# Layer norms centre half of their columns on VectorE, weight casts are queued behind the norm's last copy, and the first tile's transposes come one stretch of products later

## The chip, the cores and the metric

The kernel runs on one core of a Trainium2 chip. The metric is the device time of one execution in microseconds; the times shown are a median of three runs. One further execution was recorded by the hardware profiler, and every duration below is from that one.

## The reference

Two transformer blocks run one after the other on 256 tokens of width 1024, all in float32:

- Block 1: RMS norm, one wide input projection, three kinds of attention (sliding window, top-k sparse, memory cross attention), a gated merge, the output projection, then RMS norm, an MLP with squared ReLU (1024 to 4096 to 1024), and a final RMS norm.
- Block 2, layer A: feed-forward (SwiGLU, 1024 to 2816 to 1024), layer norm, a chunked gating unit ("sgu"), layer norm, feed-forward, layer norm. Layer B: keys and values of sparse attention are made ("kv"), feed-forward, layer norm, sparse attention ("nsa"), layer norm, feed-forward, layer norm.

```python
def layer_norm(x, g, b):
    mu = jnp.mean(xf, axis=-1, keepdims=True)
    var = jnp.mean(jnp.square(xf - mu), axis=-1, keepdims=True)
    y = (xf - mu) * lax.rsqrt(var + LN_EPS)
    return y * g + b

def post_norm(x, sub, g, b):
    return layer_norm(DN_ALPHA * x + sub, g, b)
```

Each sublayer of block 2 ends in `post_norm`, six in all; the last one is the output.

## The kernel before

**Numbers.** Every product is made of three: a float32 operand is split into a high part `h` (cast to fp32r, on ScalarE) and a low part `l` (the rest, subtracted on VectorE), and `mm3` (L273) multiplies h·h, h·l and l·h on TensorE.

**Weights.** `Stream` (L95) brings 512 KB halves of weight blocks through five raw buffers, on SP's DMA queue. `prep` (L130) casts a half on ScalarE (L142) and then subtracts on VectorE (L149); a raw buffer comes free only when both have read it. Nine pairs of high and low buffers hold prepared halves. `pump` prepares ahead as far as it is told.

**Sublayers as generators.** The 256 tokens are two tiles of 128 rows. A sublayer is a Python generator with four stops before its last products: it asks for its first weights; it makes its first products for row tile 0; the same for row tile 1; then all its middle (from `W.pump()` on), up to the last products. `down_last` (L313) makes those for one row tile: first the older weight blocks over all 1024 columns, then the last two blocks in three stretches, columns 0 to 511, 512 to 767 and 768 to 1023, so that the norm's statistics can begin on the first columns. A stretch of 256 columns is 12 products.

**The boundary.** `weave` (L426) binds the end of one sublayer, the norm and the beginning of the next. `A(t)` is the norm of row tile t, `B(t)` its transposes (TensorE, L799, two of 128x128 for each 256 columns) with the split of the result into `xT` (ScalarE L331, VectorE L332). Its order for TensorE is written by hand up to the end of the previous sublayer: last products of tile 0, then those of tile 1, in which `B(0)` is put in where `down_last` yields. After that a planner with its own model of costs orders each engine, and `A` and `B` have a higher priority than what is around them. There are eight boundaries: two with `rms_bound` (L762, entirely on VectorE) and six with `ln_bound` (L816), of which the last has no `B`.

**The layer norm.** `A(t)` of `ln_bound` adds the residual and takes statistics on VectorE in three column groups, makes -mean (L831) and the root's input (L832), and then, while VectorE computes the inverse root in small steps (`rsqrt`, L336), ScalarE subtracts the mean (L835) and GpSimd multiplies by the gain (L836), 256 columns at a time. VectorE then multiplies by the root and adds the bias (L850). In all but the last norm all four groups of columns go that way; in the last, three do and one is centred by VectorE (L840), inside the root, in steps that `rsqrt` takes from the generator `centre`.

**What is queued behind what.** The middle of the next sublayer is traced inside `issue_after(end.ins)` (L446). `end` is the last instruction of `B(1)`, VectorE's L332, and `issue_after` puts every instruction that the block traces on that instruction's engine behind it. ScalarE's instructions of the block have no such edge. The block's ScalarE instructions are the weight casts from the third weight block on, the activations, and the DMAs issued on ScalarE's queue: among them the sgu's `sgu_w_s` (L929, 512 KB, transposed by TensorE at L933 right after the first row products) and the small weights `cmp_w2` of the kv stage (L1067, L1069).

Of the kernel before, what the change touches and what calls it, by code (L numbers as in the profile page):

```python
# [23 lines left out]
F32 = mybir.dt.float32  # L24
# [42 lines left out]
def consts():  # L67
    f = np.float32
    p = np.arange(128)[:, None]
    j = np.arange(128)[None, :]  # L70
    cols, parts, n = {}, [], 0
    tri = np.where(j <= p, 0.0, BIG)
    upper = np.where(j > p, 0.0, BIG)
    dist = 255 - np.arange(384)
    nf = np.maximum(dist, 1).astype(f)
    large = 16 + (np.log(nf / f(16)) / f(math.log(8)) * f(16)).astype(np.int32)
    bucket = np.where(dist < 16, dist, np.minimum(large, 31))
    hot = np.zeros((128, 384))
    hot[:32] = (np.arange(32)[:, None] == bucket[None, :]) & (dist >= 0)[None, :]
    for name, a in (  # L80
        ("ident", p == j),
        ("tril_t", p <= j),
        ("rowok", p <= 96),
        ("swa", np.concatenate([tri, upper, tri], 1)),
        ("causal", np.concatenate([tri, np.zeros((128, 128)), tri], 1)),
        ("inv", np.power(10000.0, -np.arange(32) / 32.0)[None, :].repeat(128, 0)),
        ("hot", hot),
    ):
        cols[name] = (n, n + a.shape[1])
        parts.append(a.astype(f))  # L90
        n += a.shape[1]
    return np.ascontiguousarray(np.concatenate(parts, 1)), cols
# [84 lines left out]
class Ker:  # L177
# [135 lines left out]
    def down_last(self, ws, hs, acc, t):  # L313

        ts = slice(t * 128, (t + 1) * 128)
        m = len(ws) - 2
        for w, (hh, hl) in zip(ws[:m], hs):
            self.down(w, hh, hl, acc, t, False, False)
        if t:
            self.W.pump(2)  # L320
        for n, c0, c1 in ((0, 0, 512), (1, 0, 256), (1, 256, 512)):
            ns = slice(n * 512 + c0, n * 512 + c1)
            for i, (w, (hh, hl)) in enumerate(zip(ws[m:], hs[m:])):
                for k, (wh, wl) in enumerate(w):
                    self.mm3(acc[t][n][:, c0:c1], hh[:, k, ts], hl[:, k, ts], wh[:, 0, ns], wl[:, 0, ns], False,
                             i == 1 and k == 1, skip_group_check=c0 > 0)
            if t and n == 0:
                yield

    def split(self, h, l, x):  # L330
# [95 lines left out]
    def weave(self, prev, A, B, nxt):  # L426

        with self.manual(mybir.EngineType.PE):
            next(prev)
            self.first(A, 0)  # L430
            next(prev)
            self.first(B, 0)
            next(prev)
        if nxt:
            next(nxt)
        self.first(A, 1)
        if nxt:
            next(nxt)
        end = self.first(B, 1)
        if not nxt:  # L440
            return
        next(nxt)
        if self.dry:
            next(nxt)
        else:
            with self.tc.issue_after(end.ins):  # L446
                next(nxt)

    def first(self, f, t):
# [340 lines left out]
    def cols(self, rows, t, x):  # L790

        nc = self.nc
        xh, xl = x
        ts = slice(t * 128, (t + 1) * 128)
        for h in range(4):
            ps = self.bank()
            for j in range(2):
                k = 2 * h + j
                nc.tensor.transpose(ps[:, j * 128:(j + 1) * 128], rows[:, k * 128:(k + 1) * 128], self.ident)  # L799
            ks = slice(2 * h, 2 * h + 2)  # L800
            end = self.split(xh[:, ks, ts], xl[:, ks, ts], ps[:, :256].rearrange("p (k s) -> p k s", k=2))
        return end

    def bcast(self, row, name):
# [11 lines left out]
    def ln_bound(self, R, acc, layer, i, scale, last=False):  # L816

        nc, I = self.nc, self.I
        X = self.big([128, 2, D])
        xT = None if last else self.new_xT()  # L820
        gB, bB = (self.bcast(I[v][layer, i:i + 1], n) for v, n in (("ln_g_2", "gB"), ("ln_b_2", "bB")))

        def A(t):
            x = X[:, t]

            def part(c0, c1):
                nc.vector.scalar_tensor_tensor(x[:, c0:c1], R[:, t, c0:c1], ALPHA / scale,
                                               acc[t][c0 // 512][:, c0 % 512:(c1 - 1) % 512 + 1], op0=OP.mult, op1=OP.add)

            mv, nh, nm = self.stats(x, D, part), self.small(name="nh"), self.small(name="nh")  # L830
            nc.vector.tensor_scalar(nm, mv[:, 0:1], -1.0, None, op0=OP.mult)  # L831
            nc.vector.tensor_scalar(nh, mv[:, 1:2], -0.5 * NR, -0.5 * NR * LN_EPS / scale ** 2, op0=OP.mult, op1=OP.add)  # L832
            m = 3 if last else 4
            for cs in self.cuts[:m]:
                nc.scalar.activation(x[:, cs], x[:, cs], AF.Identity, bias=nm)  # L835
                nc.gpsimd.tensor_mul(x[:, cs], x[:, cs], gB[:, cs])  # L836

            def centre():
                for cs in self.cuts[m:]:
                    nc.vector.scalar_tensor_tensor(x[:, cs], x[:, cs], mv[:, 0:1], gB[:, cs], op0=OP.subtract,  # L840
                                                   op1=OP.mult)
                    yield

            y, = self.rsqrt([nh], centre())
            for j, cs in enumerate(self.cuts):
                if last and (t == 0 or j >= 3):
                    nc.scalar.activation(x[:, cs], x[:, cs], AF.Copy, scale=y)
                    nc.gpsimd.tensor_add(x[:, cs], x[:, cs], bB[:, cs])
                else:
                    nc.vector.scalar_tensor_tensor(x[:, cs], x[:, cs], y, bB[:, cs], op0=OP.mult, op1=OP.add)  # L850
                if last and j % 2:
                    hs = slice(j * 256 - 256, j * 256 + 256)
                    nc.sync.dma_start(self.out[0, t * 128:(t + 1) * 128, hs], x[:, hs])

        def B(t):
            if not last:
                return self.cols(X[:, t], t, xT)

        return A, B, X, xT

    def ffn(self, x, layer, i, acc, hooks={}):
# [706 lines left out]
def program(nc, arrays, stop=None):  # L1568
    aps = {}
    for name, a in arrays.items():  # L1570
        aps[name] = nc.dram_tensor(f"in_{name}_dram", a.shape, mybir.dt.from_np(a.dtype), kind="ExternalInput").ap()
    out = nc.dram_tensor("out_0_dram", (1, S, D), F32, kind="ExternalOutput").ap()
    _, cols = consts()
    C = aps.pop("consts")
    specs = Ker(Null(), Null(), aps, C, cols, out, None).run(stop)
    with tile.TileContext(nc) as tc:
        Ker(tc, nc, aps, C, cols, out, specs).run(stop)
# [11 lines left out]
```

## Time and profile before

| | |
|---|---|
| median of 3 runs | 1503.89 us (1502.61 to 1505.08) |
| the profiled execution | 1501.12 us, span 1499.2 us |
| TensorE (PE) busy | 97% of the span |
| VectorE (DVE), ScalarE (ACT), GpSimd (POOL) busy | 64%, 50%, 4% |
| granted TensorE clock, mean | 0.995 of full speed |

In the rows, PE is a product and PEld its weight load; L-numbers are lines of the kernel; an arrow `out<-in` gives the names of the tiles; a bracket at the end of a row of a timeline is the idle time of the engine before it and what ended it. A row with x4 merges four instructions of one kind, and its duration goes from the start of the first to the end of the last. "ACTq" is an instruction that ScalarE's sequencer issues, such as a DMA.

The boundaries with a norm and transposes lie at about 228, 412, 602, 750, 942, 1183 and 1295 us; the last norm is the end of the program.

### The profile page before, as it was taken

The numbers are of one execution on the slowest core, as the hardware profiler recorded it, in microseconds if no ns is written. First come the engines' busy times: TensorE is split into PE (matmuls) and PEld (weight loads), VectorE is DVE, ScalarE is ACT, GpSimd is POOL, SyncE is SP. The second block draws the span as 40 slices with busy tenths as digits, with TensorE's granted clock in tenths as the row PEclk, the third lists the DMA queues.
The fourth block names the chain that finished last, engine by engine and source line by source line (L and its number), as shares of the span: only waits on it lengthen the run. The fifth ranks groups of instructions, "written<-read, shape, count | busy, mean of one in ns | idle before, by whom it ended". The sixth has DMA issues, their size and how long they took to land.

```text
span 1499.2 us, 25253 instructions
## 1 busy us (share of the span) xinstructions
PE 1449.9 (97%) x10093; PEld 1331.4 (89%) x10093; DVE 960.0 (64%) x1608; ACT 747.5 (50%) x1149; POOL 54.3 (4%) x71
## 2 busy tenths in 40 slices
PE   6899999999999999999999999999999999999997
PEld 6688988989899999799889999899999798799996
DVE  7884398555584455877785545876645688665545
ACT  5565565444454443544354443564544487454442
POOL 0000000000000000100010000100000111100002
PEclk9999999999999999999999999999999999999999
DMA  8453276665566665577556665466766352185650
GB/s 295 128 160 91 75 243 225 224 193 185 155 198 194 184 186 165 180 222 246 159 185 186 187 193 173 146 192 218 236 194 186 109 180 85 58 265 180 187 169 29
DMA packets 191714, 264.81 MB, mean 177 GB/s; under 512 B 11024, under 2 KB 159852, under 8 KB 191596
## 3 DMA queue, kind: packets, MB, share of 16 engines
q1 hardware_dynamic: 183068, 249.56, 53.1%
q10 hardware_dynamic: 8528, 13.64, 2.9%
q8 instruction: 79, 1.29, 0.4%
q14 instruction: 39, 0.32, 0.1%
HBM read 262.09 MB, written 1.07 MB: 176 GB/s over the span
## 4 chain that ended last, share of the span: by engine, by line
PE 83%; DVE 8%; ACT 4%; DMA 3%; issue 1%; POOL 0%; ACTq 0%; DVEq 0%; SPq 0%
PE acc L311 20%; PE u L275 17%; PE u L277 17%; PE u L276 17%; DVE wl L149 3%; ACT wh L142 2%; PE acc L276 2%; PE acc L277 2%; PE acc L275 2%; PE acc L695 2%; DVE big L850 1%; PE u L799 1%; DMA wr<-in_ffn_w_dram 1%; PE acc L681 1%; PE u L1516 1%
## 5 line engine op out<-in xcount | busy, mean ns | idle before, releaser
L149 DVE TENSOR_TENSOR wl<-wr,wh 128x1024 fp32r<-128x1024 f32 (+3 forms) x488 | 572.0, 1183 | 417.5 <-ACT wh L142 415.2
L142 ACT CAST wh<-wr 128x1024 fp32r<-128x1024 f32 (+3 forms) x488 | 493.3, 1018 | 562.9 <-PE u L276 225.0
L275 PE MATMUL u<-big,wh 128*128 128x256 f32 x1960 | 551.4, 281 | 1.6 <-ACT med L412 1.1
L277 PE MATMUL u<-big,wl 128*128 128x256 f32 x1960 | 550.0, 281 | 0.0
L276 PE MATMUL u<-big,wh 128*128 128x256 f32 x1960 | 549.6, 280 | 0.0
L275 PEld LDWEIGHTS u<-big,wh 128*128 128x128 f32 x1960 | 369.3, 188 | 4.8 <-ACT med L412 1.3
L276 PEld LDWEIGHTS u<-big,wh 128*128 128x128 f32 x1960 | 368.4, 188 | 2.2
L277 PEld LDWEIGHTS u<-big,wl 128*128 128x128 f32 x1960 | 369.0, 188 | 0.0
L311 PE MATMUL acc<-wh,t 128*128 128x512 f32 x928 | 263.9, 395 | 0.0
L311 PEld LDWEIGHTS acc<-wh,t 128*128 128x128 f32 x928 | 169.8, 188 | 34.9
L311 PE MATMUL acc<-wl,t 128*128 128x512 f32 x464 | 145.6, 394 | 0.0
L311 PEld LDWEIGHTS acc<-wl,t 128*128 128x128 f32 x464 | 87.1, 188 | 20.5
L275 PE MATMUL u<-wh,big 128*128 128x256 f32 (+1 forms) x304 | 101.6, 334 | 0.5 <-ACT t L1429 0.5
L277 PE MATMUL u<-wh,big 128*128 128x256 f32 (+1 forms) x304 | 101.1, 333 | 0.0
L276 PE MATMUL u<-wl,big 128*128 128x256 f32 (+1 forms) x304 | 100.4, 330 | 0.0
L836 POOL TENSOR_TENSOR big<-big,med 128x256 f32<-128x256 f32 x46 | 38.1, 859 | 1387.4 <-ACT big L835 1354.0
L331 ACT CAST t<-t 128x512 fp32r<-128x512 f32 x66 | 41.0, 621 | 56.1 <-DVE t L536 24.3
L275 PEld LDWEIGHTS u<-wh,big 128*128 128x128 f32 x304 | 57.8, 190 | 6.8 <-ACT t L1429 0.9
L277 PEld LDWEIGHTS u<-wh,big 128*128 128x128 f32 x304 | 57.7, 190 | 5.5
L276 PEld LDWEIGHTS u<-wl,big 128*128 128x128 f32 x304 | 57.8, 190 | 5.3
L332 DVE TENSOR_TENSOR t<-t,t 128x512 fp32r<-128x512 f32 x66 | 45.4, 687 | 14.3 <-ACT t L331 14.3
L276 PE MATMUL acc<-wl,t 128*128 128x512 f32 (+1 forms) x168 | 53.9, 321 | 0.3 <-DVE wl L149 0.3
(256 smaller groups left out, 1365.5 us busy)
## 6 DMA issues: line engine op xcount, KB each, us to landing
wr<-in_ffn_w_dram SPq DMA_DIRECT2D x264, 512.0 KB, 4.3
wr<-in_w_in_dram SPq DMA_DIRECT2D x34, 512.0 KB, 3.9
wr<-in_w_mlp_in_dram SPq DMA_DIRECT2D x32, 512.0 KB, 4.5
wr<-in_w_mlp_out_dram SPq DMA_DIRECT2D x32, 512.0 KB, 4.2
wr<-in_sgu_w_in_dram SPq DMA_DIRECT2D x32, 512.0 KB, 4.9
wr<-in_sgu_w_out_dram SPq DMA_DIRECT2D x16, 512.0 KB, 4.7
wr<-in_kv_w_dram SPq DMA_DIRECT2D x12, 512.0 KB, 4.0
wr<-in_w_out_dram SPq DMA_DIRECT2D x8, 512.0 KB, 4.6
```

The costliest lines, as they stand in the source:

```text
L142: self.nc.scalar.copy(h, v)
L149: self.nc.vector.tensor_sub(l, v, h.bitcast(F32))
L275: mm(out, lh, rh, start=start, stop=False, **k)
L276: mm(out, lh, rl, start=False, stop=False, **k)
L277: mm(out, ll, rh, start=False, stop=stop, **k)
L311: mm(acc[t][n], a[:, k, ts], b[:, 0, n * 512:(n + 1) * 512], start=s, stop=e)
L331: self.nc.scalar.copy(h, x)
L332: return self.nc.vector.tensor_sub(l, x, h.bitcast(F32))
L681: nc.tensor.transpose(pt[:, c:c + 128], e[:, c:c + 128], self.ident)
L695: nc.tensor.matmul(out, PT[:, c:c + 128], v(b), start=b == 0, stop=b == nb - 1)
L799: nc.tensor.transpose(ps[:, j * 128:(j + 1) * 128], rows[:, k * 128:(k + 1) * 128], self.ident)
L836: nc.gpsimd.tensor_mul(x[:, cs], x[:, cs], gB[:, cs])
```

## The change

Three edits. In `ln_bound` the first two groups of 256 columns are centred and multiplied by the gain on VectorE, inside the root, and the last two go over ScalarE and GpSimd, in all six norms. `cols` returns both last instructions of `B(t)`, ScalarE's copy and VectorE's subtraction, and `weave` queues the block behind both, each on its engine. `down_last` yields one stretch of 12 products later, so that `B(0)` stands between columns 512 to 767 and 768 to 1023 of tile 1.

```diff
@@ down_last
-            if t and n == 0:
+            if t and n and not c0:
                 yield
@@ weave
-            with self.tc.issue_after(end.ins):
+            with self.tc.issue_after(end[0].ins), self.tc.issue_after(end[1].ins):
                 next(nxt)
@@ cols
-            end = self.split(xh[:, ks, ts], xl[:, ks, ts], ps[:, :256].rearrange("p (k s) -> p k s", k=2))
+            p, h, l = ps[:, :256].rearrange("p (k s) -> p k s", k=2), xh[:, ks, ts], xl[:, ks, ts]
+            end = [nc.scalar.copy(h, p), nc.vector.tensor_sub(l, p, h.bitcast(F32))]
         return end
@@ ln_bound
-            m = 3 if last else 4
-            for cs in self.cuts[:m]:
+            for cs in self.cuts[2:]:
                 nc.scalar.activation(x[:, cs], x[:, cs], AF.Identity, bias=nm)
                 nc.gpsimd.tensor_mul(x[:, cs], x[:, cs], gB[:, cs])
             def centre():
-                for cs in self.cuts[m:]:
+                for cs in self.cuts[:2]:
                     nc.vector.scalar_tensor_tensor(x[:, cs], x[:, cs], mv[:, 0:1], gB[:, cs], op0=OP.subtract,
                                                    op1=OP.mult)
                     yield
```

## Rows read from the trace of the kernel before

**Rows 1.** The page: the chain that ended last, by engine.

```profile
PE 83%; DVE 8%; ACT 4%; DMA 3%; issue 1%; POOL 0%; ACTq 0%; DVEq 0%; SPq 0%
```

**Rows 2.** Waits of PE, whole kernel: total us, times, longest.

```profile
PE u L799 <- DVE big L850: 13.2, 24, 1.2
...
PE u L799 <- DVE med L781: 1.5, 1, 1.5
```

**Rows 3.** Timeline, PE, first tile of a layer norm: start us, us, instruction.

```profile
750.28 0.41 PE L799 MATMUL u<-cst,big 128*128 128x128 f32 x2 [0.64 <-DVE big L850]
751.15 1.20 PE L799 MATMUL u<-cst,big 128*128 128x128 f32 x6 [0.46 <-DVE big L850]
752.10 0.36 PE L275 MATMUL acc<-wh,t 128*128 128x256 f32 x1
...
754.90 0.28 PE L277 MATMUL acc<-wh,t 128*128 128x256 f32 x1
```

**Rows 4.** Timeline, DVE, both tiles of that norm.

```profile
746.64 1.23 DVE L149 TENSOR_TENSOR wl<-wr,wh 128x1024 fp32r<-128x1024 f32 x1
...
749.29 2.50 DVE L850 SCALAR_TENSOR_TENSOR big<-big,nwy,med 128x256 f32<-128x256 f32 x4
...
755.22 0.75 DVE L827 SCALAR_TENSOR_TENSOR big<-big,acc 128x256 f32<-128x256 f32 x2 [0.90 <-PE acc L277]
...
756.94 0.15 DVE L831 TENSOR_SCALAR nh<-bmv 128x1 f32<-128x1 f32 x1
...
759.32 3.06 DVE L850 SCALAR_TENSOR_TENSOR big<-big,nwy,med 128x256 f32<-128x256 f32 x4 [0.77 <-POOL big L836]
...
764.01 1.22 DVE L149 TENSOR_TENSOR wl<-wr,wh 128x1024 fp32r<-128x1024 f32 x1
```

**Rows 5.** Timeline, POOL, second tile of that norm.

```profile
758.54 3.16 POOL L836 TENSOR_TENSOR big<-big,med 128x256 f32<-128x256 f32 x4 [7.83 <-ACT big L835]
```

**Rows 6.** Timeline, ACT, second tile of that norm.

```profile
754.16 3.90 ACT L142 CAST wh<-wr 128x1024 fp32r<-128x1024 f32 x4 [1.40 <-PE acc L277]
757.96 1.71 ACT L835 ACTIVATE big<-big,nh 128x256 f32<-128x256 f32 x4
...
763.27 0.37 ACT L331 CAST big<-u 128x256 fp32r<-128x256 f32 x1 [0.32 <-PE u L799]
```

**Rows 7.** Timeline, PE, second tile, and the next products with fresh weights.

```profile
760.40 0.41 PE L799 MATMUL u<-cst,big 128*128 128x128 f32 x2 [1.10 <-DVE big L850]
...
769.34 0.37 PE L275 MATMUL u<-big,wh 128*128 128x256 f32 x1
```

**Rows 8.** Timeline, PE, first tile of the first RMS norm.

```profile
229.38 1.60 PE L799 MATMUL u<-cst,med 128*128 128x128 f32 x8 [1.45 <-DVE med L781]
```

**Rows 9.** Timeline, DVE, first tile of the second RMS norm.

```profile
411.94 1.67 DVE L781 SCALAR_TENSOR_TENSOR big<-big,nwy,med 128x256 f32<-128x256 f32 x4
```

**Rows 10.** Timeline, ACT, after the first RMS norm.

```profile
241.09 0.45 ACTq L929 DMA_DIRECT2D med<-in_sgu_w_s_dram  x1
```

**Rows 11.** DMA issues: times, KB each, median us to landing.

```profile
med<-in_g_final_dram ACTq DMA_DIRECT2D x1, 512.0 KB, 3.4
...
med<-in_sgu_b_s_dram ACTq DMA_DIRECT2D x1, 512.0 KB, 7.2
```

**Rows 12.** Timeline, PE, sgu after its first row products.

```profile
621.40 1.04 PE L933 MATMUL u<-cst,med 128*128 128x128 f32 x8
```

**Rows 13.** Windows, after the transposes of two norms: engines' busy us (x), PEclk.

```profile
763.50:769.00 5.50, 5.50 (x50) 5.50 (x49) 5.33 (x7) 2.10 (x4) 0.00 (x0) 1.00 0.38 114
956.00:962.20 6.20, 6.20 (x45) 6.20 (x45) 5.79 (x6) 1.20 (x3) 0.00 (x0) 0.79 0.42 126
```

**Rows 14.** Timeline, DVE, the last norm, second tile.

```profile
1491.61 0.48 DVE L840 SCALAR_TENSOR_TENSOR big<-big,bmv,med 128x256 f32<-128x256 f32 x1
...
1493.71 0.65 DVE L351 SCALAR_TENSOR_TENSOR nwy<-nwa,nwy 128x1 f32<-128x1 f32 x1
```

**Rows 15.** Timeline, ACT, the beginning of the program.

```profile
6.55 0.91 ACTq L1067 DMA_DIRECT2D w<-in_cmp_w_dram  x2
```

## The prediction

> **What bounds the kernel now.** The chain of waits comes first: TensorE holds 83% of it [rows 1], so time is won only where TensorE stands still or where its work is cut, and this change cuts none. The second view is therefore the list of TensorE's waits. Of everything it waits for, the transposes that wait for the layer norm's last product (L850) are the longest entry: 13.2 us in 24 waits, five boundaries with two tiles each, so about 2.6 us a boundary; the first RMS norm adds 1.5 us [rows 2]. Nothing else that the change touches is in that list with as much. The third view is the timeline of one boundary, the norm at 750 us, as the model of all five. In the first tile TensorE stands still 0.64 us before the first pair of transposes and 0.46 us before the second [rows 3], since VectorE begins L850 only at 749.29 and needs 2.50 us for four [rows 4]. In the second tile it waits 1.10 us before the first pair [rows 7] and less before the next ones; there L850 itself has waited 0.77 us for GpSimd and then goes at GpSimd's pace, 3.06 us against 3.16 us [rows 4, 5]. GpSimd was late because ScalarE was: four weight casts end at 758.06, while the mean was there at 756.94 [rows 4, 6].
>
> **The change, part by part.** All sums are against the profiled execution, 1501.12 us (its span is 1499.2 us); the median of the runs shown is 2.8 us above it, and I carry the difference over to that.
>
> *Transposes a stretch later.* The stretch is 12 products. 24 of them stand between 752.10 and 754.90 with the last starting there, 2.80 / 23 = 0.12 us each, so 1.4 us of work now fills TensorE's wait in the first tile [rows 3]. At a layer norm this wait costs 0.64 + 0.46 = 1.1 us idle. TensorE would come to the transposes at about 750.9 instead of 749.5. The data of the last pair is there at 749.29 + 2.50 = 751.8 today. With the second edit the root comes a little later and the four L850 go faster (below), so I keep 751.8 for the last pair. TensorE then waits 0 to 0.5 us, and the first tile gives about 0.9 us, bounds 0.6 and 1.1. In the first RMS norm the whole wait of 1.45 us is covered [rows 8]; VectorE has other work next, so I take 1.3 (bounds 0.6 and 1.45). In the second RMS norm no wait stands in the list, so it gives nothing, plus or minus 0.3.
>
> *Half of the centring on VectorE.* It adds two multiplications a tile, 0.48 us each (L840, the same instruction in the last norm) [rows 14], and takes away half of ScalarE's and GpSimd's chain. With the other engines quiet four such products take 1.67 us [rows 9], beside GpSimd 2.50 and 3.06 [rows 4]. In the last norm, where one group is already centred on VectorE, the root is there at 1493.71 + 0.65 = 1494.36, 2.75 us after L840 begins [rows 14], 2.9 with the step for -mean before it (0.15) [rows 4]. I take the same 2.9 for two groups: one more product costs 0.5, and GpSimd, which stretched the last small step to 0.65, is done sooner. Then -mean to the last product is 2.9 + 1.7 = 4.6 us, against 759.32 + 3.06 - 756.94 = 5.4 today [rows 4]: 0.8 us gained in the second tile, bounds -0.5 and 1.2. In the first tile the chain is longer, because a weight subtraction of 1.23 us stands inside the root (746.64) [rows 4]. Whether the planner leaves it there, once the centring fills the holes, cannot be read here: it stays in the forecast.
>
> *What VectorE can hand on.* Between the two tiles VectorE is idle only for 0.90 us, waiting for TensorE's last columns [rows 4]. The first tile brings these columns 0.9 us earlier or more, and VectorE can use 0.6 of it before its own queue is the limit. So -mean of the second tile comes 0.6 earlier and the last product 0.6 + 0.8 = 1.4 us earlier. After it TensorE has the same work as before, or more where the planner puts the transposes later among the products, which hides wait. Bounds 0.6 (nothing but the idle time closes) and 2.6 (all of the wait goes); I take 1.7, nearer the sum than the ends. Four boundaries give 6.8 us. The one before sparse attention has other VectorE work in between and waited less; I take 1.3. Together 8.1 us.
>
> *Casts behind the norm's copies.* In the second tile this frees ScalarE for L835 at once: the gain is already in the 1.4. The price: the four casts at 754.16 and the one before them now start after the last copy, at 763.27 + 0.37 [rows 6], about 1.5 us sooner in the new time. Cast (3.90 / 4 = 1.0) and subtraction (1.22) follow. Today VectorE begins these subtractions at 764.01, itself held back by the norm, and TensorE needs the first at 769.34 [rows 4, 7], so 4.1 us are spare after 765.2. The new order eats about 1.0 for the cast and the 1.7 by which TensorE comes sooner; 1.4 remain. Each further half needs 1.2 us of VectorE and feeds TensorE for 24 x 0.12 = 2.8. The raw buffers come free with the subtraction and not with the cast, so SP's queue of loads shifts by the same 1 us. I cost it at nothing; without that cover it would be about 1 us a boundary.
>
> *The DMAs in the block.* ScalarE's queue also carries the load of `sgu_w_s`: today issued at 241.09, 380 us ahead [rows 10]; now behind the copy at about 614, and behind the two casts that are ahead of it in the program. Similar loads land after 3.4 to 7.2 us [rows 11]. TensorE is at its transposes at 621.40 today [rows 12], some 2 us earlier then, so they are missed by up to 5 us, or by nothing where the planner puts row products before them. I take 1.2 us (bounds 0 and 4), since the planner knows of the wait but not its length. *The Trainium skill (DMA: Bandwidth & Descriptors, Rules for kernel authors) says to issue a DMA early and wait late; its fit in the section on the anatomy of one DMA, about 2 us and the bytes at 436 GB/s, makes 3.2 us an estimate for 512 KB, by which this term would be 0. The row with 7.2 us speaks against so short a time.* The small weights at 6.55 move away too [rows 15], from a stretch in which DMAs are awaited: 0 to 0.5 gained, 0.3 taken.
>
> *The clock.* After the transposes of the norm at 942 us the granted clock fell to the lower level in part of a stretch (mean 0.79; 45 products in 6.20 us against 50 in 5.50), after a boundary in which TensorE stood still; at the others it did not [rows 13]. 45 products take 4.95 us there, so 1.25 us were lost. I count half of it, 0.6, as given back by shorter waits.
>
> *The end.* In the last norm VectorE centres two groups instead of one: +0.5, less what GpSimd no longer stretches (a small step of 0.65 [rows 14], where the like of it, L831, takes 0.15 [rows 4]); -0.3 to +0.5, taken as 0.2 lost.
>
> Sum: 1.3 + 8.1 - 1.2 + 0.3 + 0.6 - 0.2 = 8.9 us. 1501.1 - 8.9 = 1492.2, and 1495.0 against the median.
>
> **The rivals.**
>
> *All of the wait goes (1490).* The subtraction falls out of the first tile's root, 1.2 us sooner, and the planner, which sees VectorE as late, sets the second transposes after more row products. Then four boundaries give 2.6, the fifth 2.0, the RMS norm 1.4, the clock 1.2: 15.0 - 1.2 = 13.8. For it: the centring fills the holes into which it was put. Against: that cast is ready at just that time.
>
> *The wait is handed on (1502).* TensorE comes sooner to the second tile, but VectorE does not: only 0.6 of idle time closes. Five times 0.6, 0.6 in the RMS norm, less 1.2 for the load: 2.4, so 1501.5. For it: VectorE has only 0.90 us idle between the tiles. Against: L850 waits for GpSimd and ScalarE today, not for VectorE.
>
> *The load of `sgu_w_s` is waited for in full (1498).* 4 instead of 1.2 us; it decides if the transposes keep their place in TensorE's order.
>
> *VectorE becomes the bound (slower, 1508).* Both centring products run beside GpSimd and take its pace, 3.06 / 4 = 0.77 rather than 0.42, and the weight subtraction of 1.23 us stands in both tiles' roots. The second tile's chain is then 2 x 0.77 + 1.23 = 2.8 us longer, less the 1.4 that the faster L850 gives back (3.06 - 1.67): last products 1.4 later, and 0.6 sooner from the idle time, so 0.8 lost at five boundaries, 4.0; with the load's 1.2 and the RMS norm's 1.3 gained, 3.9 over the median. It decides once the centring and what stands in the root add over 2 us. Against it: casts no longer come in the second tile, so there is little to subtract. *The Trainium skill (SBUF — State Buffer, Who interferes with whom) says that a VectorE instruction with two SBUF inputs and a GpSimd one that reads SBUF shut each other out for whole instructions; L850 beside L836 agrees. By it the second centring product of each tile would wait out a GpSimd product.*
>
> **How the numbers follow.** Forecast, 1491 to 1499 alone: 0.50. All of it goes: 0.20. Handed on: 0.15. The load in full: 0.08. VectorE the bound: 0.07. The range of 1488 to 1502.5 leaves out that last case and tails. What a measurement here can tell from no change is 0.2%, 3.0 us. Faster: 0.48 + 0.20 + 0.07 + a third of 0.15 = 0.80; the same: 0.10 of the wait handed on and 0.03 of the others, 0.13; slower: 0.07.
>
> **What would show it.** TensorE's waits on L850 fall from 13.2 to about 5 us, the first tile's nearly to none; no cast stands on ScalarE between the second tile's -mean and its last copy; L836 stands twice a tile, and L850 does not wait for it. L929 is issued after 600 us, with or without an idle TensorE before L933. The prediction is wrong if waits on L149 appear after the row products, if the second tile's waits are longer than today's, or if more than one further stretch shows the lower clock.

## The result and the profile after

The changed kernel takes 1488.34 us (median of four runs, 1486.28 to 1489.05) against 1503.81 us of the kernel before in the same comparison (four runs): ratio 0.9895, 95% interval 0.9878 to 0.9912, so 15.5 us or 1.05% less. The forecast was 1495.0 with a range of 1488 to 1502.5: the direction and the mechanism hold, the gain is under-estimated by 6.6 us, and the time lies 0.3 us above the lower end of the range. The profiled execution took 1489.02 us, 12.1 less than the one of before; the other 3.4 us of the medians lie between the executions (see the clock, below). One of the eleven runs of the kernel with the casts queued alone took 6273.75 us, and that kernel's ratio and clock below leave it out.

The page's chain, and TensorE's waits over the whole kernel (total us, times, longest), as in [rows 1, 2]:

```profile
PE 82%; DVE 10%; ACT 3%; issue 2%; DMA 2%; POOL 0%; ACTq 0%; DVEq 0%; POOLq 0%
```

```profile
PE u L799 <- DVE big L850: 5.0, 5, 1.2
...
PE u L497 <- DVE t L536: 3.2, 3, 2.7
...
PE acc L276 <- DVE wl L149: 1.1, 3, 0.7
```

The wait for the last product falls from 13.2 us in 24 to 5.0 in 5, one for each second tile; the first RMS norm's 1.5 us [rows 2] is gone. The same boundary as in [rows 3, 7], TensorE, now at 747 us:

```profile
747.20 0.28 PE L277 MATMUL acc<-wh,t 128*128 128x256 f32 x1
747.31 1.08 PE L799 MATMUL u<-cst,big 128*128 128x128 f32 x8
748.15 0.36 PE L275 MATMUL acc<-wh,t 128*128 128x256 f32 x1
...
755.34 0.41 PE L799 MATMUL u<-cst,big 128*128 128x128 f32 x2 [1.14 <-DVE big L850]
...
755.74 0.41 PE L799 MATMUL u<-cst,big 128*128 128x128 f32 x2
```

The first tile's eight transposes have no bracket; the second tile has one. Line numbers differ a little from kernel to kernel: L832 is L831 of before, L828 is L827, L802 is L331 and L332, and the last products are on L849, L850 or L851. VectorE, both tiles, as in [rows 4]:

```profile
742.23 0.15 DVE L832 TENSOR_SCALAR nh<-bmv 128x1 f32<-128x1 f32 x1
...
746.17 1.67 DVE L850 SCALAR_TENSOR_TENSOR big<-big,nwy,med 128x256 f32<-128x256 f32 x4
...
750.40 0.74 DVE L828 SCALAR_TENSOR_TENSOR big<-big,acc 128x256 f32<-128x256 f32 x2
...
752.12 0.15 DVE L832 TENSOR_SCALAR nh<-bmv 128x1 f32<-128x1 f32 x1
...
752.70 0.48 DVE L840 SCALAR_TENSOR_TENSOR big<-big,bmv,med 128x256 f32<-128x256 f32 x1
...
753.40 0.40 DVE L351 SCALAR_TENSOR_TENSOR nwy<-nwa,nwy 128x1 f32<-128x1 f32 x1
...
754.52 0.16 DVE L351 SCALAR_TENSOR_TENSOR nwy<-nwa,nwy 128x1 f32<-128x1 f32 x1
754.71 1.67 DVE L850 SCALAR_TENSOR_TENSOR big<-big,nwy,med 128x256 f32<-128x256 f32 x4
```

GpSimd and ScalarE, second tile, as in [rows 5, 6]:

```profile
752.89 1.57 POOL L836 TENSOR_TENSOR big<-big,med 128x256 f32<-128x256 f32 x2 [6.97 <-ACT big L835]
```

```profile
752.30 0.91 ACT L835 ACTIVATE big<-big,nh 128x256 f32<-128x256 f32 x2 [3.37 <-DVE nh L832]
...
757.39 0.37 ACT L802 CAST big<-u 128x256 fp32r<-128x256 f32 x1 [0.44 <-PE u L799]
757.66 2.01 ACT L142 CAST wh<-wr 128x1024 fp32r<-128x1024 f32 x2
```

ScalarE starts 0.18 us after -mean, no cast stands before the last copy, GpSimd is done at 754.46, and L850 waits for nobody and takes 1.67 us instead of 3.06 [rows 4]. The idle 0.90 us before the last columns [rows 4] are gone as well: the row at 750.40 has no bracket.

One number sums up a boundary: **the norm's length**, from the start of the first tile's -mean to the end of the second tile's last product, all on VectorE. It is 756.38 - 742.23 = 14.15 us, against 759.32 + 3.06 - 745.81 = 16.57 before (the row of the first -mean is below; the rest in [rows 4]). VectorE, kernel before:

```profile
745.81 0.15 DVE L831 TENSOR_SCALAR nh<-bmv 128x1 f32<-128x1 f32 x1
```

Over the five boundaries it falls from 82.6 to 70.9 us, by 11.7. By the places of TensorE's products in the two traces (read to some 0.3 us each, so that the sum is 12.3), the 12.1 us are: the layer norms at 602, 750, 942, 1183 and 1295 us -2.6, -2.4, -4.2, -2.1, -2.3; the RMS norms -1.8 and -0.5; the end -0.4; lost again +1.2 in the first 226 us, +1.4 in a stretch at the lower clock at 991 us, and +1.4 in L497's waits and around them (3.2 us in the list, 1.8 before). The 4.2 at 942 us holds some 1.3 us of the lower-clock stretch of [rows 13], which is not there in this execution.

### The profile page after: what moved, and what is told of

Same layout as the page of the kernel before. It is cut to its first block, busy times and chain, and to the rows that moved or that the text cites. A ratio compares the mean times of both kernels' runs of the same rounds, so it can differ in the third digit from the quotient of the medians.

```text
span 1487.2 us, 25225 instructions
## 1 busy us (share of the span) xinstructions
PE 1446.4 (97%) x10093; PEld 1334.0 (90%) x10093; DVE 957.4 (64%) x1630; ACT 736.1 (49%) x1127; POOL 40.1 (3%) x49
## 4 chain that ended last, share of the span: by engine, by line
PE 82%; DVE 10%; ACT 3%; issue 2%; DMA 2%; POOL 0%; ACTq 0%; DVEq 0%; POOLq 0%
PE acc L311 21%; PE u L275 17%; PE u L276 17%; PE u L277 17%; DVE wl L149 3%; PE acc L276 2%; PE acc L695 2%; PE acc L277 2%; PE acc L275 2%; ACT wh L142 1%; DVE big L850 1%; DVE bst L379 1%; PE acc L681 1%; DVE big L828 1%; PE u L799 1%
## 5 line engine op out<-in xcount | busy, mean ns | idle before, releaser
L149 DVE TENSOR_TENSOR wl<-wr,wh 128x1024 fp32r<-128x1024 f32 (+3 forms) x488 | 573.2, 1184 | 419.0 <-ACT wh L142 406.6
L331 ACT CAST t<-t 128x512 fp32r<-128x512 f32 x66 | 41.0, 621 | 56.5 <-DVE t L536 25.3
L836 POOL TENSOR_TENSOR big<-big,med 128x256 f32<-128x256 f32 x24 | 23.2, 985 | 1389.2 <-ACT big L835 1355.7
L332 DVE TENSOR_TENSOR t<-t,t 128x512 fp32r<-128x512 f32 x66 | 45.4, 688 | 14.9 <-ACT t L331 14.9
```

Source lines behind the costliest of these rows:

```text
L149: self.nc.vector.tensor_sub(l, v, h.bitcast(F32))
L331: self.nc.scalar.copy(h, x)
L332: return self.nc.vector.tensor_sub(l, x, h.bitcast(F32))
```

## The experiments

The comparison that every run shares is with the kernel before (medians 1503.1 to 1504.3 us there). The ratio is that of the means, so it can differ by a us from the medians given below. "Products" is how many products of the next sublayer's rows the planner puts between the second tile's last products and its transposes at the 750 us boundary; "norm" is the norm's length there; "waits" are TensorE's for L850 and L781 together; "clock" is the mean granted clock over the timed runs.

| kernel | ratio, 95% interval | norm us | products | waits us | clock |
|---|---|---|---|---|---|
| before | 1 | 16.57 | 35 | 15.0 | 0.9945 |
| the change | 0.9895 [0.9878, 0.9912] | 14.15 | 37 | 5.3 | 0.9968 |
| transposes later alone | 0.9960 [0.9948, 0.9971] | 15.38 | 35 | 9.9 | 0.9933 |
| centring alone | 0.9956 [0.9944, 0.9968] | 15.50 | 37 | 10.3 | 0.9958 |
| casts queued alone | 1.0011 [1.0002, 1.0020] | 15.96 | 32 | 15.1 | 0.9936 |
| without the later transposes | 0.9946 [0.9933, 0.9959] | 15.02 | 37 | 8.3 | 0.9954 |
| without the centring | 0.9974 [0.9966, 0.9983] | 15.09 | 32 | 11.8 | 0.9919 |
| without the queued casts | 0.9895 [0.9881, 0.9910] | 14.31 | 37 | 6.1 | 0.9948 |
| one group on VectorE | 0.9934 [0.9921, 0.9946] | 14.70 | 34 | 8.8 | 0.9954 |
| three groups | 0.9899 [0.9886, 0.9913] | 14.37 | 42 | 3.3 | 0.9952 |
| four groups | 0.9878 [0.9863, 0.9893] | 13.94 | 46 | 0.5 | 0.9965 |
| transposes behind the last products | 0.9892 [0.9878, 0.9907] | 14.12 | 35 | 2.7 | 0.9975 |
| the same, three groups | 0.9893 [0.9876, 0.9909] | 13.84 | 37 | 0.0 | 0.9958 |
| three groups, casts not queued | 0.9897 [0.9879, 0.9915] | 14.51 | 42 | 3.7 | 0.9958 |

**Each edit alone.** First the later transposes:

```diff
-            if t and n == 0:
+            if t and n and not c0:
                 yield
```

> The kernel before with the transposes of the first tile one stretch later, and nothing else. Theory (each wait is won where it stands): TensorE's wait at the first tile goes, 1.1 us idle at each of five layer norms and 1.5 us at the first RMS norm, 4 to 6 us under the kernel before, 1498 to 1500 us; the waits of the second tile stay as they are, about 1.7 us idle each. Rival (the wait is handed on): VectorE and GpSimd reach the second tile no sooner, its waits grow by what the first tile saved, and the time is 1502 to 1504 us.

Measured 1496.86 us, 7.0 less by the medians and 6.0 by the ratio: its twelve runs reach from 1494.76 to 1505.00. Then the centring:

```diff
-            m = 3 if last else 4
-            for cs in self.cuts[:m]:
+            for cs in self.cuts[2:]:
...
-                for cs in self.cuts[m:]:
+                for cs in self.cuts[:2]:
```

> The kernel before with two of four column groups centred on VectorE, and nothing else. Theory: in the first tile the last L850 ends 0.4 us sooner after -mean, in the second 1.2 us sooner; the casts still stand ahead of ScalarE's mean subtraction, but only two groups wait for it: 4 to 6 us gained, 1498 to 1500 us, with the transposes' waits at about half of 13.2 us. Rival (VectorE is the bound): the two products more lengthen the root at both tiles and the time stays within 2 us of before.

Measured 1497.44 us, 6.4 less, a little more than the theory's 4 to 6; the rival falls. And the casts behind the copies:

```diff
-            with self.tc.issue_after(end.ins):
+            with self.tc.issue_after(end[0].ins), self.tc.issue_after(end[1].ins):
...
+            end = [nc.scalar.copy(h, p), nc.vector.tensor_sub(l, p, h.bitcast(F32))]
```

> The kernel before with the block queued behind ScalarE's last copy too, and nothing else. Theory: ScalarE is free when the second tile's -mean is there, GpSimd starts 0.9 us sooner at five norms, and L850 goes at GpSimd's pace as before: 3 to 5 us gained, 1499 to 1501 us; the load of sgu_w_s is issued after 600 us and costs nothing. Rival (the order of the casts is a matter of the gap only as long as GpSimd does all columns; the root itself then holds L850): under 1 us, 1503 to 1504 us. Second rival: the later casts make TensorE wait for weights after the row products, 1505 us or more.

Measured 1505.7 us, 1.8 more than before's 1503.86: no gain, so the theory falls. The second rival's 1505 came, but not its cause: the waits on L149 are 1.0 us, 0.7 of them at 16 us and the rest at 220, none behind a layer norm. What the 1.8 us are isn't shown.

In the first of the three, the first tile's wait goes, as the theory had it, but against it part of that comes back at the second: GpSimd still makes four products there, and TensorE, which comes sooner, waits 1.75 us for them instead of 1.10 [rows 7]. GpSimd, VectorE and TensorE, second tile, later transposes alone:

```profile
756.17 2.97 POOL L836 TENSOR_TENSOR big<-big,med 128x256 f32<-128x256 f32 x4 [6.41 <-ACT big L835]
```

```profile
757.72 2.49 DVE L850 SCALAR_TENSOR_TENSOR big<-big,nwy,med 128x256 f32<-128x256 f32 x4
```

```profile
758.70 0.41 PE L799 MATMUL u<-cst,big 128*128 128x128 f32 x2 [1.75 <-DVE big L850]
```

With centring alone the last products (L849 there) take 1.67 us in both tiles, but the first tile's wait stays (0.73 us), and so does the RMS norm's. The weight casts still stand before ScalarE's subtraction there, so GpSimd works beside the last steps of the root, and these are long: the chain from -mean to the last product is 4.75 us, only 0.7 less than before where the theory had 1.2, against 4.26 in the changed kernel. GpSimd and VectorE, second tile, centring alone:

```profile
760.06 1.42 POOL L835 TENSOR_TENSOR big<-big,med 128x256 f32<-128x256 f32 x2 [8.67 <-ACT big L834]
```

```profile
760.24 0.57 DVE L348 SCALAR_TENSOR_TENSOR nwa<-nwa 128x1 f32<-128x1 f32 x1
760.85 0.65 DVE L351 SCALAR_TENSOR_TENSOR nwy<-nwa,nwy 128x1 f32<-128x1 f32 x1
```

The casts alone do shorten the norm, by 0.6 us, but the planner spends it: it now puts 32 products ahead of the transposes instead of 35, three products of 0.12 us less of cover, and TensorE comes to them sooner and waits 1.32 us, no shorter than before. TensorE, second tile, casts alone:

```profile
762.54 0.41 PE L799 MATMUL u<-cst,big 128*128 128x128 f32 x2 [1.32 <-DVE big L851]
```

**Each edit taken out.** In each run one of the diffs above is undone and the other two stay. First without the later transposes:

> The changed kernel with the transposes of the first tile where they were. Theory: centring and order stay, TensorE comes to the first tile's transposes 1.4 us sooner and waits there again, about 0.7 us at five norms and 1.5 at the first RMS norm; 5 to 7 us over the changed kernel, 1493 to 1495 us. Rival (the stretch only moves a wait from one tile to the other): within 2 us of the changed kernel.

Measured 1495.06 us, 6.7 more: the theory holds, the rival falls. The first tiles wait 0.7 us again and the first RMS norm 1.8; the second tiles wait less (0.65 us at 750 us, for 1.14), since TensorE comes to them later. The casts' place does show here: the chain in the second tile is 4.28 us, against 4.75 with centring alone, and the waits are 8.3 us for 10.3. TensorE, first tile, without the later transposes:

```profile
750.18 1.59 PE L799 MATMUL u<-cst,big 128*128 128x128 f32 x8 [0.72 <-DVE big L850]
```

Then without the centring:

> Later transposes and casts behind the copies, without the centring on VectorE. Theory (the order of the casts pays only together with the centring: alone it cost 1.6 us, with the centring it gave 2.4): the two parts add, -7.0 + 1.6 = -5.4, so about 1498.5 us (1497.0 to 1500.0), and the second tiles still wait about 1.3 to 1.7 us before their first pair, since four products on GpSimd set the pace of L850 (3.1 us for four). Rival (the order needs the later transposes to pay, not the centring): about 1494 us, and the second tile's first wait falls below 1.2 us.

Measured 1500.86 us: 0.9 above the theory's range and by the medians 4.0 more than the later transposes alone (1496.86), though the intervals of the two ratios overlap. By the ratios the parts do add, as the theory says: 0.9960 + 0.0011 = 0.9971, and 0.9974 is measured. The norm is 0.3 us shorter than with the later transposes alone, but again with 32 products for 35, so the wait is 1.82 us for 1.75. Of the 1.9 us by which all waits are longer, 1.4 stand at the first RMS norm, where this kernel's VectorE had first waited 1.51 us for a weight cast. TensorE and VectorE there, without the centring:

```profile
232.18 1.60 PE L799 MATMUL u<-cst,med 128*128 128x128 f32 x8 [1.42 <-DVE med L781]
```

```profile
223.60 1.23 DVE L149 TENSOR_TENSOR wl<-wr,wh 128x1024 fp32r<-128x1024 f32 x1 [1.51 <-ACT wh L142]
```

The clock (0.9919, the lowest of all) may make the rest; that isn't shown. The rival (1494) falls. Last, without the queued casts:

> Later transposes and centring on VectorE, with the weight casts and the loads as before. Theory (order is worth 2.4 us on top of centring, whatever the transposes do): 1490.7 us (1489.5 to 1492.0); ScalarE's L835 of the second tile starts up to 1 us after -mean behind a cast at some boundaries, and L850 waits for GpSimd there; the load of sgu_w_s goes out early again. Rival (with the later transposes VectorE is late anyway, so a late L835 costs nothing): 1488 us, as with all three.

Measured 1489.15 us, ratio 0.9895: not to be told from all three (the waits are 0.8 us longer). The theory (the casts' place is worth 2.4 us) falls, the rival holds. In the length of the norm the later transposes (-1.2) and the centring (-1.1) add to -2.3 (14.31), and the casts' place takes 0.16 more. ScalarE starts 0.48 us after -mean here, behind the casts, but with only two subtractions and two products to follow VectorE hardly notices. ScalarE, then VectorE, second tile, without the queued casts:

```profile
753.86 0.93 ACT L834 ACTIVATE big<-big,nh 128x256 f32<-128x256 f32 x2
```

```profile
753.38 0.15 DVE L831 TENSOR_SCALAR nh<-bmv 128x1 f32<-128x1 f32 x1
...
756.14 1.67 DVE L849 SCALAR_TENSOR_TENSOR big<-big,nwy,med 128x256 f32<-128x256 f32 x4
```

**How many groups on VectorE.** One, three and four of the four, all three edits kept; for one:

```diff
-            for cs in self.cuts[2:]:
+            for cs in self.cuts[1:]:
...
-                for cs in self.cuts[:2]:
+                for cs in self.cuts[:1]:
```

> All three edits, but one column group of four is centred on VectorE and three on ScalarE and GpSimd. Theory (the last product is set by the root plus four L850 at whichever pace GpSimd leaves): the root comes 0.48 us sooner, but GpSimd's third product ends about 3.1 us after -mean, so the L850 beside it take 0.77 us each; last product 4.2 to 4.6 us after -mean against 4.26; time 1488 to 1491 us. Rival (every VectorE instruction beside GpSimd is stretched, the small steps of the root too): 5.0 us after -mean, +0.7 at five boundaries, 1492 us or more.

Measured 1494.17 us. The theory's 4.2 to 4.6 us for the chain is right (4.60), its time is not; the rival's time and its stretched small steps came, but not its chain of 5.0. The root comes later with one product in it than with two: 759.33 - 756.40 = 2.93 us against 754.71 - 752.12 = 2.59. VectorE, second tile, one group:

```profile
756.40 0.16 DVE L832 TENSOR_SCALAR nh<-bmv 128x1 f32<-128x1 f32 x1
...
757.42 0.52 DVE L351 SCALAR_TENSOR_TENSOR nwy<-nwa,nwy 128x1 f32<-128x1 f32 x1
...
758.28 0.34 DVE L348 SCALAR_TENSOR_TENSOR nwa<-nwa 128x1 f32<-128x1 f32 x1
758.65 0.65 DVE L351 SCALAR_TENSOR_TENSOR nwy<-nwa,nwy 128x1 f32<-128x1 f32 x1
759.33 1.67 DVE L850 SCALAR_TENSOR_TENSOR big<-big,nwy,med 128x256 f32<-128x256 f32 x4
```

GpSimd's third product, to 757.18 + 2.10 = 759.28, runs beside the last step of the root, which takes 0.65 us instead of 0.16. GpSimd, second tile, one group:

```profile
757.18 2.10 POOL L836 TENSOR_TENSOR big<-big,med 128x256 f32<-128x256 f32 x3 [6.77 <-ACT big L835]
```

With 34 products for 37 this gives 0.34 + 0.36 = 0.7 us at five boundaries, 3.5 in all: the waits' 8.8 for 5.3. The other 2.3 of the 5.8 us may go with the mean clock (0.9954 for 0.9968); that isn't shown.

> All three edits, but three column groups of four are centred on VectorE and one on ScalarE and GpSimd. Theory (VectorE's own queue sets the last product once GpSimd is done before the root): one more product of 0.48 us inside the root, less what GpSimd's missing second product no longer stretches; last product 4.5 to 4.7 us after -mean against 4.26, five boundaries and the end: 1490 to 1491.5 us. Rival (what GpSimd stretched is as much as the product costs): 4.2 us after -mean, 1488 us.

Measured 1488.48 us: the same as with two groups, and the rival's time. The chain is 4.42 us, between theory and rival, but the planner puts 42 products ahead of the transposes and the waits fall by 2.0 us. Why the time doesn't fall with them isn't shown; the clock is lower (0.9952 for 0.9968).

> All three edits, but all four column groups are centred on VectorE; ScalarE and GpSimd have no part in the norms with transposes (in the last norm only its first tile keeps them). Theory (what the root costs is its small steps beside GpSimd, 0.34 to 0.66 us instead of 0.16, not the products): no step above 0.3 us, the root 2.8 us after -mean, last product 4.5 us after it against 4.26 with two groups and 4.42 with three; 1488 to 1490 us. Rival (each product moved to VectorE costs its 0.48 us): 5.2 us after -mean, +0.9 at five boundaries and the end, 1493 us or more.

Measured 1485.29 us, below the theory's 1488 and the fastest of all. VectorE, second tile, then TensorE, four groups:

```profile
751.01 0.15 DVE L832 TENSOR_SCALAR nh<-bmv 128x1 f32<-128x1 f32 x1
...
752.57 0.15 DVE L351 SCALAR_TENSOR_TENSOR nwy<-nwa,nwy 128x1 f32<-128x1 f32 x1
752.64 0.48 DVE L840 SCALAR_TENSOR_TENSOR big<-big,bmv,med 128x256 f32<-128x256 f32 x1
...
753.34 0.16 DVE L348 SCALAR_TENSOR_TENSOR nwa<-nwa 128x1 f32<-128x1 f32 x1
753.53 0.16 DVE L351 SCALAR_TENSOR_TENSOR nwy<-nwa,nwy 128x1 f32<-128x1 f32 x1
753.73 1.67 DVE L850 SCALAR_TENSOR_TENSOR big<-big,nwy,med 128x256 f32<-128x256 f32 x4
```

```profile
754.36 0.41 PE L799 MATMUL u<-cst,big 128*128 128x128 f32 x2
```

With GpSimd out of it no small step is stretched, so four products cost 4.39 - 4.26 = 0.13 us more of chain than two, and the first tile's comes out 0.2 us shorter. The planner, which counts four products on VectorE, puts 46 products ahead of the transposes, and the wait for the last products is gone: no bracket (0.9 us of waits for the split L802, at the last pairs, are new). Against the change it is 0.9878 to 0.9895, and the intervals overlap; the runs themselves hardly do (1483.16 to 1486.35 against 1486.28 to 1489.05). That it beats the change is likely, not settled.

**Transposes behind all of the second tile's last products.**

```diff
-            if t and n and not c0:
-                yield
+        if t:
+            yield
```

> All three edits, but the first tile's transposes stand one more stretch later, behind all of the second tile's last products. Theory (the second tile waits for VectorE because its last columns and the first tile's split come together there; TensorE's 1.08 us of transposes now fill the 1.0 us that is left of that wait, and the columns come 1.1 us sooner): L850 waits fall from 5.0 to about 1 us, 1483 to 1486 us. Rival (VectorE has no idle time from the first tile's products on, so its split only moves from before -mean to behind it, into the root or in front of the first row products): waits stay 4 to 6 us or turn into waits for L802, 1488 to 1491 us.

Measured 1486.95 us, ratio 0.9892: between the ranges of theory and rival, and not to be told from the change. What the rival says of the waits holds: L850's waits fall to 2.7 us, but the first row products now wait for the first tile's split, which follows on VectorE too late. TensorE's waits and TensorE at the boundary, this kernel:

```profile
PE u L799 <- DVE big L850: 2.7, 5, 0.7
PE u L275 <- DVE big L802: 2.7, 6, 0.6
```

```profile
750.42 0.38 PE L275 MATMUL u<-wh,big 128*128 128x256 f32 x1 [0.43 <-DVE big L802]
```

> As the one before, with three column groups on VectorE. Theory (three groups cost 0.16 us of chain but leave less wait in the planner's order, 2.8 instead of 5.0 us): 1482 to 1486 us if the later place pays, else as that one within 1.5 us. Rival (VectorE is the bound in the order of the last stretch, and the third product adds to it): 1 to 3 us more than with two groups.

Measured 1486.68 us, as the one before within 1.5 us: the alternative that the theory left. L850 is no longer waited for at all, L802 for 2.9 us.

> Later transposes and three column groups on VectorE, weight casts and loads as before. Theory (with the last norm's ScalarE part down to one group, a cast ahead of it costs nothing, so the casts' place is worth nothing): 1487 to 1489 us. Rival (a cast of 1.0 us ahead of the one L835 makes GpSimd late): 1490 us or more, with L850 waiting for L836.

Measured 1488.37 us, against 1488.48 with the queued casts: the theory holds. A cast before the one subtraction costs 0.14 us of norm and nothing that the times can tell.

## Why the prediction was right, and where its sizes failed

*Bound and mechanism: right.* TensorE's idle time at the boundaries was nearly the whole gain (the end gave 0.4); the first tile's wait closed, GpSimd's pace left L850, VectorE's idle time before the last columns closed.

*First RMS norm, 1.3:* 1.8 measured, the whole wait of 1.45 and some 0.3 more; the second gave 0.5 where nothing was put down. That no wait stands in the list for it was misread: there are 0.3 us, before and after (for L781, at its second tile). The 0.5 came elsewhere: its first tile's eight transposes take 1.50 us before (at 412.68) and 1.03 after (at 413.50), without a bracket in either.

*Layer norms, 8.1: the term that was mis-sized.* They gave 2.6 + 2.4 + 2.9 + 2.1 + 2.3 = 12.3 us (the 942 us one without the clock's 1.3). Two of its steps were too small. The chain from -mean to the last product, 4.6 us there, is 4.26, since the root comes after 2.59 us and not 2.9. That 2.9 was borrowed from the last norm, where GpSimd has three products and stretches the last step to 0.65 [rows 14]; with two it is done, and the step takes 0.16. And "VectorE can use 0.6 of it": the second -mean comes 752.12 - 742.23 = 9.89 us after the first, 11.13 before [rows 4], so 1.24 sooner. The idle 0.90 closes in full, and the first tile's faster L850 brings 0.37 more (5.61 us from -mean to its end, 5.98 before), which the sum had left out because it held the first tile's end at its old place. 1.24 + 1.18 = 2.4 us a boundary, in place of the sum of 1.4 and of the 1.7 taken. The bound of 2.6, "all of the wait goes", was no bound: 602 us gave 2.6 and 942 us 2.9, with 0.9 and 1.2 us of wait still standing. It came from the brackets, and these show less than TensorE loses: a bracket begins at the end of a product's row, 0.28 us after its start, while products follow each other every 0.12 us [rows 3]. By the starts, the first tile cost 1.8 us and not 0.64 + 0.46. TensorE, kernel before, ahead of the first row of [rows 3]:

```profile
749.02 0.40 PE L276 MATMUL acc<-wl,t 128*128 128x512 f32 x1
749.25 0.39 PE L277 MATMUL acc<-wh,t 128*128 128x512 f32 x1
```

From 749.25 to the next product at 752.10 [rows 3] it is 2.85 us, of which 0.23 are that product and 0.84 eight transposes without a wait (747.31 to 748.15, after). So the step that TensorE stands still 1.1 us in the first tile, of which 0.9 are won, was too small as well: the whole 1.8 went, and the other 0.6 of the 2.4 came at the second tile.

*Where the sum was too simple.* It took a shorter norm as time gained. The casts alone shorten the norm and gain nothing; what TensorE loses is the wait that is left after the products which the planner puts ahead. Those went from 35 to 37 with the change, which the prediction left open ("as before, or more").

*Casts at nothing:* right within 1 us; the waits on L149 are 1.1 us, in three, at 16 and 219 us and none behind a layer norm. But beside the other two edits this one gives nothing that the times can tell either (0.8 us of waits), though part of the gain was put to it ("frees ScalarE for L835 at once"). It does shorten the chain where the transposes are not later (4.28 us for 4.75).

*Load of `sgu_w_s`, -1.2:* 0. ACTq and TensorE, after:

```profile
612.62 0.39 ACTq L929 DMA_DIRECT2D med<-in_sgu_w_s_dram  x1
```

```profile
617.82 1.03 PE L933 MATMUL u<-cst,med 128*128 128x128 f32 x8
```

Issued 5.2 us ahead, it was there in time: no bracket. *The page-based estimate in the prediction (3.2 us, by the Trainium skill, DMA: Bandwidth & Descriptors, its section on the anatomy of one DMA) had the term at 0, and this row doesn't contradict it. The page gives that fit for DMAs that GpSimd issues, while this one goes out on ScalarE's queue.*

*Start, +0.3:* 1.2 us were lost in the first 226 us of the profiled execution, although a stretch at the lower clock that the kernel before has from 16.5 to 19.9 us (0.50 of full speed) isn't there any more. At 60 us the kernels with the queued casts stand -1.2 to +1.7 us against before, those without -1.3 to +1.6, so it can't be put down to the moved loads; what it is stays open.

*The end, -0.2:* +0.4. From -mean to L850 it is 2.57 us now, 3.00 before, for the same reason as in the second tiles.

*The clock, +0.6.* Between the profiles nothing at the boundaries: the lower-clock stretch at 955 us is gone, with the 1.3 us that it cost, and one at 991 us is new and costs 1.4. It begins while TensorE stands still for 2.73 us, waiting for L497's input; the same wait was 1.84 us before, and the clock didn't fall there:

```profile
991.41 0.91 PE L497 MATMUL u<-cst,t 128*128 128x128 f32 x3 [2.73 <-DVE t L536]
```

Windows of the two, after (PEclk is the granted clock; the lower level is 0.50 of full speed):

```profile
948.00:954.20 6.20, 6.20 (x55) 6.20 (x54) 6.04 (x9) 5.58 (x7) 0.00 (x0) 1.00 0.43 127
988.00:994.40 6.40, 3.67 (x20) 3.47 (x20) 5.11 (x7) 3.05 (x5) 0.00 (x0) 0.73 0.71 227
```

Over all timed runs the mean granted clock was 0.9968 in the changed kernel's four and 0.9945 in 23 runs of the kernel before; over 1500 us of a TensorE-bound program 0.0023 are some 3.4 us, an estimate. The two profiled executions stood at 0.996 and 0.995, which leaves about 2 us of that for the 3.4 between 12.1 and 15.5. And such estimates are good to a few us only: the kernel without the queued casts (0.9948) should by the same sum be 3.0 us slower than the change, and is 0.8 slower. Why one kernel has more such stretches than another isn't settled: two kernels with long second-tile waits have the lowest means (0.9919 and 0.9933), but the casts' edit alone (0.9936) has the waits of before, and one group on VectorE has waits as long (1.86 us) at 0.9954.

*The rivals.* "All of the wait goes" (1490) is nearer in number, but not by its mechanism: the subtraction L149 stays in the first tile's root, and one wait a boundary stays. "Handed on" names what happens, in part, where the later transposes stand without the centring. "VectorE the bound": its condition, two centring products at GpSimd's pace, did not come, since GpSimd starts at 752.89, when the second (752.70) is half done.

## What to carry to other kernels

Before a chain on one engine is shortened, ask what that engine's neighbour does to its smallest steps: here giving VectorE more work and GpSimd less made VectorE's own chain shorter (4.60 us with one product, 4.26 with two, 4.42 with three, 4.39 with all four). And where a planner fills a wait with other work by its own model, count the filling after the change: time is won only if the wait that remains gets shorter, and a norm 0.6 us shorter with three products less in front won nothing. An early end in one tile is handed on in full to the next only if the engine between them has idle time or gets faster too; add both. And what an engine loses at a wait is read from the starts of its instructions before and behind it, not from the bracket alone.

## What the runs showed of the hardware

Beside a running GpSimd multiplication VectorE's steps on 128x1 took 0.34 to 0.71 us instead of 0.16 (L348, L351), and the 128x256 products 0.62 to 0.77 instead of 0.42 each; L344 took 0.27 us with and without it. A centring product that had begun before GpSimd did kept its 0.48 us (L840 at 752.70, after). *The Trainium skill (SBUF — State Buffer, Who interferes with whom) says that a VectorE instruction with two SBUF inputs shuts out, and is shut out by, a GpSimd one that reads SBUF, while one with a single input doesn't contend, outside the modes of VectorE that use two ports. The rows agree in the kinds: L351 and L348 are of the form with two tensors, L344 of the form with one.* That a step of 0.16 us can cost four times as much was known from [rows 14]; that this makes one group on VectorE slower than two was not expected.
